# Conv stage of a two-layer decoder trunk: unit 3's weights made between the tiles of operand 6, and the squares of tiles 4 to 7 formed in pairs behind products 5 to 9

## The chip, the cores and the metric

The kernel runs as one program on one core of a Trainium2 chip. The metric is device time in microseconds (us), the median over runs. Before the change three runs took 2207.89, 2202.42 and 2208.22 us, so the median is 2207.89 us.

## What is computed

The reference is a decoder trunk of two layers in float32, with 1024 positions and a model width of 1024. The first layer mixes with a short gated convolution, the second with dilated attention, and a SwiGLU network follows each. Cut to what matters here:

```python
def rms_norm(x, g):
    y = x * lax.rsqrt(jnp.mean(x * x, axis=-1, keepdims=True) + EPS)
    return y * g

def short_conv_mixer(h, w_in, conv_k, w_out):
    b, c, u = jnp.split(h @ w_in, 3, axis=-1)
    y = depthwise_causal_conv(c * u, conv_k)          # 3 taps
    return (b * y) @ w_out

for i in range(2):
    h = rms_norm(x, mix_norm[i])
    x = x + (short_conv_mixer if i == 0 else dilated_attention)(h, ...)
    h = rms_norm(x, ffn_norm[i])
    x = x + (silu(h @ w_gate[i]) * (h @ w_up[i])) @ w_down[i]
return rms_norm(x, final_norm)
```

## The kernel before

**Operands.** Activations lie transposed: x is eight tiles X[0] to X[7] of 128 features by 1024 positions, each in two halves of 512 positions. Every float32 operand of a matmul is split in two: ScalarE makes the high half (a rounded copy, L138 for weights, L541 and L847 for activations) and VectorE the low half (the value minus the high half, L139, L542, L848). A product is taken as high times high, high times low, low times high, so each pair of 128-row blocks costs three matmuls of 128 by 512 (L549, L550, L551). The third of the three is the first that reads the weight's low half.

**Products.** The conv layer's first projection, x times `conv_w_in`, is done as Strassen products: unit u stands for a block of output columns, and for each unit seven products m = 1 to 7 are formed over four blocks of rows (12 matmuls). A method `products` walks a list of (unit, m) and records the matmuls; below, product n is the n-th of this list, counted from 0: (0,1) (1,1) (0,2) (1,2) (2,1) (2,2) (3,1) (3,2) (4,1) (4,2) (0,6) (1,6) (0,7) (1,7) (0,5) (1,5) (0,4) (1,4) (0,3) (1,3) (2,6) (2,5) (2,7), and so on. So product 6 is (3,1), 8 is (4,1), 10 to 13 are (0,6) (1,6) (0,7) (1,7), and 20 is (2,6). Products 1, 6, 7 and 4 of one unit add up in one PSUM bank. Behind m = 1, 6 and 7 the bank's value up to then is copied out by ScalarE (`save`, L555, written `part<-bank` in the profile), and the next product of that unit may not write to the bank before the copy is done.

**The order.** The schedule is the order of the code: each engine does its instructions in the order in which they are recorded. After product n is recorded, `start(n)` in `Conv.mix` records whatever else is put behind it: `ensure(self.at(u, m))` makes the split weights for everything up to (u, m), `combos` forms sums of weight blocks on VectorE (L186), `next(prep)` goes one step on in the generator `operands`, which makes the activation operands 1, 2, 6, 7, 5, 4, 3 (operand 6 is made in four tiles, two in each of two steps: L868, L869, L541, L542), and `self.squares` is the norm's share.

**The norm.** The products are formed with x that is only multiplied by the gain; the division by the root mean square comes later, so the sums of squares are needed only for what follows product 20. `summed` (L416 to L428) squares half a tile of X on ScalarE: tiles 0 and 1 go straight into two accumulators (L423), the others into a page `sq` (L427), and a DMA issued by GpSimd adds that half page to one of the two accumulators (L428, even tiles to one, odd tiles to the other). Two such DMAs on the same half of the same accumulator wait for one another. Hooks behind product 20 (`gather`) add the two accumulators on VectorE (`joined`, L431) and sum over the features with 16 small matmuls against ones (L461); those stand on TensorE between product 20 and product 21. `spread` behind (2,7) makes the scale.

Tiles live in 41 shared pages of 128 by 1024; a page that is taken again waits until its last reader is done, DMAs included. In the version before, the squares of tiles 0 to 3 are recorded behind product 0 (first half) and 4 (second half); those of tiles 4 to 7 stand in the list `late`, one half tile behind each product from 10 to 17. Unit 3's weights, `w<-raw` for (3,1) and (3,2), are made behind product 3, after all four tiles of operand 6.

Of the kernel before, what the change touches and what calls it, by code (L numbers as in the profile page):

```python
# [21 lines left out]
KT = D // 128  # L22
# [72 lines left out]
def trunk(ctx: ExitStack, tc: tile.TileContext, x, gains_in, cwi, ck, cwo, wqkv, wo, relb,  # L95
# [63 lines left out]
    def ensure(upto):  # L159
        while op_state[0] < min(upto + 1, len(ops)):  # L160
            key = ops[op_state[0] + 1][0] if op_state[0] + 1 < len(ops) else None
            if key in sums_of:
                sums_of.pop(key)()
            made[op_state[0]] = ops[op_state[0]][1]()
            op_state[0] += 1
# [191 lines left out]
    def run(*gens):  # L357
        for _ in zip(*gens):
            pass
        for g in gens:  # L360
            for _ in g:
                pass
# [12 lines left out]
    X = [None] * KT  # L375
# [459 lines left out]
    class Conv(Strassen):  # L835
# [166 lines left out]
        def mix(self, group1):  # L1002
            norm = self.norm
            prep = self.operands()
            stats = norm.stats(0, S)
            late = [(k, h) for h in range(2) for k in range(4, KT)]

            def start(n):
                if n == 0:
                    next(prep)  # L1010
                    ensure(self.at(2, 2))
                    self.squares(range(4), 0)
                elif n == 1:
                    next(prep)
                elif n == 2:
                    self.first(0)
                    next(prep)
                elif n == 3:
                    self.first(1)
                    ensure(self.at(3, 2))  # L1020
                    combos[CONV, 0](6)
                    ensure(self.at(4, 2))
                elif n == 4:
                    ensure(self.at(0, 6))
                    combos[CONV, 1](6)
                    ensure(self.at(1, 6))
                    self.squares(range(4), 1)
                elif n == 7:
                    next(prep)
                elif n == 8:  # L1030
                    ensure(self.at(1, 7))
                    self.first(2)
                elif n == 9:
                    self.first(3)
                    next(prep)
                    self.first(4)
                elif n == 10:
                    next(prep)
                    ensure(self.at(1, 5))
                elif n == 12:  # L1040
                    next(prep)
                    ensure(self.at(1, 4))
                elif n == 14:
                    next(prep, None)
                    ensure(self.at(1, 3))
                elif n == 18:
                    self.ahead = 3
                if n > 9 and late:
                    k, h = late.pop(0)
                    self.squares((k,), h)  # L1050
                    if h:
                        X[k] = None

            def gather():
                norm.joined()
                next(stats)

            def spread():
                run(stats)
                nc.scalar.activation(norm.acc, norm.rstd, AF.Square)  # L1060
                self.ready = True

            self.base = op_state[1]
            ensure(self.at(0, 1))
            next(prep)
            ensure(self.at(0, 2))
            self.run(start, {(2, 6): gather, (2, 7): spread})
            group1("co", self.plain, self.hid)

# [812 lines left out]
```

## Time and profile before

| what | value |
|---|---|
| median of three runs | 2207.89 us (2202.42 to 2208.22) |
| the profiled execution, its own time | 2207.41 us |
| span of the profile | 2205.6 us (1.8 us of the execution lie around it) |
| TensorE busy, share of the span | 2142.4 us, 97% |
| granted TensorE clock, mean | 0.986 of full |
| VectorE, ScalarE, GpSimd busy | 79%, 45%, 8% |
| moved over DMA | 265.03 MB, 120 GB/s on average |
| sum of squares DMAs (`acc<-sq`), conv stage | 12 of 256 KB |

All of the change lies in the first 90 us of the span. Times in the profile count from the span's start. In a timeline row stand the start, the duration, the engine, the line, the operation with its tiles, and in square brackets how long the engine stood idle before it and what ended that. PE is TensorE, DVE is VectorE, ACT is ScalarE, POOL is GpSimd, SP issues the loads.

### The profile page before, as it was taken

The page shows a single profiled execution, that of the slowest core. Times are in us where ns is not written, and L with a number is a line of the kernel's source. Part 1 is how long each engine was busy: PE and PEld are TensorE (multiplying, and loading weights), DVE is VectorE, ACT ScalarE, POOL GpSimd, SP SyncE. Part 2 cuts the span into 40 slices and gives each one's busy share as a digit, 9 for nine tenths or more (in the row PEclk, how much of TensorE's full clock was granted, in tenths as well). Part 3 has the DMA queues.
Part 4 walks back from the last instruction along what each step waited for, and adds up shares of the span by engine and source line. Part 5 has one row for each costly group of instructions (what it writes and reads, how often), then busy time and mean ns, then how long its engine had stood idle before and what let it go on. Part 6 is the DMA issues. An engine that isn't in the chain of part 4 may idle for free. (4 is left out here: it accounts for less than half of the span.)

```text
span 2205.6 us, 30628 instructions
## 1 busy us (share of the span) xinstructions
PE 2142.4 (97%) x11158; PEld 1830.9 (83%) x11158; DVE 1744.5 (79%) x3216; ACT 1000.9 (45%) x1812; POOL 180.9 (8%) x236
## 2 busy tenths in 40 slices
PE   8899999999999999999999999998999999999998
PEld 7688878778888878878999999886778888878887
DVE  7698758888888798865677777865888888889886
ACT  6433426444444544345545454534534444454435
POOL 1100001100101000010111111112000101000000
PEclk9999999999999999999999999998999999999999
DMA  5322543223233474323333333455223233265432
GB/s 183 91 74 80 204 154 86 98 94 105 106 104 112 133 269 151 111 67 132 85 91 99 93 96 99 138 168 161 71 77 103 103 106 111 99 233 194 156 93 77
DMA packets 137073, 265.03 MB, mean 120 GB/s; under 512 B 48520, under 2 KB 59800, under 8 KB 136922
## 3 DMA queue, kind: packets, MB, share of 16 engines
q1 hardware_dynamic: 75978, 184.80, 25.9%
q0 software_dynamic: 19776, 55.18, 7.7%
q10 hardware_dynamic: 41168, 23.10, 3.5%
q8 instruction: 88, 1.44, 0.3%
q14 instruction: 63, 0.52, 0.1%
HBM read 187.31 MB, written 66.27 MB: 115 GB/s over the span
## 5 line engine op out<-in xcount | busy, mean ns | idle before, releaser
L549 PE MATMUL bank<-b,w 128*128 128x512 f32 x1784 | 704.4, 395 | 16.3 <-ACT b L541 6.0
L551 PE MATMUL bank<-b,w 128*128 128x512 f32 x1784 | 700.5, 393 | 7.5 <-DVE w L139 7.5
L550 PE MATMUL bank<-b,w 128*128 128x512 f32 x1784 | 700.5, 393 | 0.6 <-DVE b L848 0.6
L549 PEld LDWEIGHTS bank<-b,w 128*128 128x128 f32 x1784 | 338.7, 190 | 91.4 <-ACT part L555 8.4
L551 PEld LDWEIGHTS bank<-b,w 128*128 128x128 f32 x1784 | 338.4, 190 | 82.5 <-DVE w L139 11.2
L550 PEld LDWEIGHTS bank<-b,w 128*128 128x128 f32 x1784 | 338.7, 190 | 70.1 <-DVE b L848 1.2
L138 ACT ACTIVATE w<-combo 128x512 fp32r<-128x512 f32 (+2 forms) x464 | 234.5, 535 | 295.5 <-DVE combo L186 287.2
L139 DVE TENSOR_TENSOR w<-combo,w 128x512 fp32r<-128x512 f32 (+2 forms) x464 | 260.2, 574 | 60.6 <-ACT w L138 58.6
L555 ACT ACTIVATE part<-bank 128x512 f32<-128x512 f32 x168 | 99.8, 594 | 263.9 <-PE bank L551 251.0
L139 DVE TENSOR_TENSOR w<-raw,w 128x512 fp32r<-128x512 f32 (+2 forms) x316 | 169.0, 559 | 16.4 <-ACT w L138 14.9
L559 DVE TENSOR_TENSOR part<-part,bank 128x256 f32<-128x256 f32 (+1 forms) x348 | 158.7, 485 | 28.3 <-PE bank L551 14.3
L138 ACT ACTIVATE w<-raw 128x512 fp32r<-128x512 f32 (+2 forms) x316 | 150.9, 520 | 47.4 <-PE bank L551 13.9
L770 DVE TENSOR_TENSOR x<-x,bank 128x512 f32<-128x512 f32 x168 | 114.2, 680 | 33.1 <-PE bank L551 32.8
L352 PE MATMUL bank<-w_hi,w 128*128 128x512 f32 (+1 forms) x320 | 121.3, 379 | 3.2 <-ACT w L138 3.2
L354 PE MATMUL bank<-w_hi,w 128*128 128x512 f32 (+1 forms) x320 | 119.1, 372 | 0.9 <-DVE w L139 0.9
L353 PE MATMUL bank<-w_lo,w 128*128 128x512 f32 (+1 forms) x320 | 118.8, 371 | 0.0
L482 DVE TENSOR_TENSOR x<-x,bank 128x512 f32<-128x512 f32 (+1 forms) x104 | 66.1, 642 | 65.5 <-PE bank L354 57.2
L352 PE MATMUL bank<-h_hi,w_hi 128*128 128x512 f32 x256 | 104.5, 408 | 0.1
L186 DVE TENSOR_TENSOR combo<-raw 128x512 f32<-128x512 f32 (+1 forms) x160 | 102.9, 643 | 0.0
L354 PE MATMUL bank<-h_hi,w_lo 128*128 128x512 f32 x256 | 100.2, 391 | 0.7 <-DVE w_lo L139 0.5
L353 PE MATMUL bank<-h_lo,w_hi 128*128 128x512 f32 x256 | 99.9, 390 | 0.0
L1156 ACT ACTIVATE part<-part 128x512 f32<-128x512 f32 x66 | 39.7, 627 | 106.0 <-DVE part L559 106.0
(258 smaller groups left out, 3854.2 us busy)
## 6 DMA issues: line engine op xcount, KB each, us to landing
hin<-part SPq DMA_DIRECT2D x126, 256.0 KB
raw<-in_ffn_w_gate SPq DMA_DIRECT2D x44, 512.0 KB
raw<-in_ffn_w_up SPq DMA_DIRECT2D x44, 512.0 KB
part<-sum POOLq DMA_DIRECT2D x72, 256.0 KB, 2.7
raw<-in_ffn_w_down SPq DMA_DIRECT2D x48, 384.0 KB
x<-spill SPq DMA_DIRECT2D x24, 512.0 KB
raw<-in_attn_w_qkv SPq DMA_DIRECT2D x24, 512.0 KB
raw<-in_conv_w_in SPq DMA_DIRECT2D x21, 512.0 KB
```

The source lines that it names most:

```text
L138: nc.scalar.activation(hi, src, AF.Copy)
L139: eng.tensor_tensor(out=lo, in0=src, in1=hi, op=ALU.subtract)
L186: eng.tensor_tensor(out=c, in0=a, in1=b, op=op)
L352: nc.tensor.matmul(b, whi[:, a], ahi[:, s], start=first, stop=False)
L353: nc.tensor.matmul(b, whi[:, a], alo[:, s], start=False, stop=False)
L354: nc.tensor.matmul(b, wlo[:, a], ahi[:, s], start=False, stop=last)
L549: nc.tensor.matmul(b, hi[:, a], bhi, start=start and k == 0, stop=False, skip_group_check=True)
L550: nc.tensor.matmul(b, hi[:, a], blo, start=False, stop=False, skip_group_check=True)
L551: nc.tensor.matmul(b, lo[:, a], bhi, start=False, stop=k == n - 1, skip_group_check=True)
L555: nc.scalar.activation(t, b, AF.Copy)
L559: nc.vector.tensor_tensor(out=t, in0=t, in1=b, op=ALU.add)
L770: nc.vector.tensor_tensor(out=X[n][:, half(h)], in0=X[n][:, half(h)], in1=b, op=ALU.add)
```

## The change

Three things in `start` of `Conv.mix` move; no arithmetic, no tile size and no DMA is added or removed. The rest of the kernel is the same, four lines shorter, so a line number above 1050 is four smaller in the changed kernel.

```diff
-            late = [(k, h) for h in range(2) for k in range(4, KT)]
-
...
                 elif n == 2:
                     self.first(0)
+                    ensure(self.at(3, 2))
                     next(prep)
                 elif n == 3:
                     self.first(1)
-                    ensure(self.at(3, 2))
                     combos[CONV, 0](6)
                     ensure(self.at(4, 2))
...
                 elif n == 14:
                     next(prep, None)
                     ensure(self.at(1, 3))
+                    X[:] = [None] * KT
                 elif n == 18:
                     self.ahead = 3
-                if n > 9 and late:
-                    k, h = late.pop(0)
-                    self.squares((k,), h)
-                    if h:
-                        X[k] = None
+                if n in (5, 6, 8, 9):
+                    self.squares(*{5: ((4, 5), 0), 6: ((6, 7), 0), 8: ((4, 5), 1), 9: ((6, 7), 1)}[n])
```

Unit 3's weights come between the second and the third tile of operand 6. On ScalarE this reads as follows; `w<-raw` are the high halves of weights (of the four in a row before, the first two are unit 3's, the others unit 4's), `b<-t_331` to `b<-t_334` the four tiles of operand 6, and the `part<-bank` at the end is the copy behind product 4.

```order
 L541 ACTIVATE b<-t_331 128x512
 L541 ACTIVATE b<-t_332 128x512
+L138 ACTIVATE w<-raw 128x512 x2
 L541 ACTIVATE b<-t_333 128x512
 L541 ACTIVATE b<-t_334 128x512
-L138 ACTIVATE w<-raw 128x512 x4
+L138 ACTIVATE w<-raw 128x512 x2
 L555 ACTIVATE part<-bank 128x512
```

The two high halves for unit 3 move ahead of two tiles, and unit 4's stay where they were. On VectorE the two low halves for unit 3 go ahead of the third and fourth tile of operand 6 too, directly behind the addition L559.

```order
 L542 TENSOR_TENSOR b<-t_331,b 128x512
 L559 TENSOR_TENSOR part<-part,bank 128x512
+L139 TENSOR_TENSOR w<-raw,w 128x512 x2
 L868 SCALAR_TENSOR_TENSOR t_329<-x,gains,t_329 128x512
 L869 SCALAR_TENSOR_TENSOR t_333<-x,gains,t_329 128x512
```

They moved past eight VectorE operations (the two L868, the two L869, three L542 and one L559); what stands behind those eight keeps its place in the list.

The squares: on ScalarE, from the squares of tiles 2 and 3 (second half) on, the kernel before has this. The three `part<-bank` rows are the copies behind products 6, 8 and 10; `b<-t_327` to `b<-t_330` are operand 7; `w<-combo` are the weights of products 12 and 13; L847 makes operand 5.

```order
L427 ACTIVATE sq<-x 128x512 x2
L555 ACTIVATE part<-bank 128x512
L541 ACTIVATE b<-t_327 128x512
L541 ACTIVATE b<-t_328 128x512
L541 ACTIVATE b<-t_329 128x512
L541 ACTIVATE b<-t_330 128x512
L555 ACTIVATE part<-bank 128x512
L138 ACTIVATE w<-combo 128x512 x2
L555 ACTIVATE part<-bank 128x512
L847 ACTIVATE b<-x,gains 128x512 x4
```

The changed kernel has this at the same place.

```order
L427 ACTIVATE sq<-x 128x512 x4
L555 ACTIVATE part<-bank 128x512
L427 ACTIVATE sq<-x 128x512 x2
L541 ACTIVATE b<-t_327 128x512
L541 ACTIVATE b<-t_328 128x512
L541 ACTIVATE b<-t_329 128x512
L541 ACTIVATE b<-t_330 128x512
L555 ACTIVATE part<-bank 128x512
L138 ACTIVATE w<-combo 128x512 x2
L427 ACTIVATE sq<-x 128x512 x4
L555 ACTIVATE part<-bank 128x512
L847 ACTIVATE b<-x,gains 128x512 x4
```

Eight half tiles of squares now stand here: two and two around the copy behind product 6, and four between the weights of product 13 and the copy behind product 10. The later places, behind products 10 to 17, are empty of squares. The eight accumulating DMAs on GpSimd keep their number and order, and GpSimd has no other work in this stage; the loads on SP keep their order.

## The prediction

> **What bounds the kernel now.** I read the page first, then the list of TensorE's waits, then the timeline of each engine over the first 90 us, and last the granted clock in windows.
>
> ```profile
> PE 2142.4 (97%) x11158; PEld 1830.9 (83%) x11158; DVE 1744.5 (79%) x3216; ACT 1000.9 (45%) x1812; POOL 180.9 (8%) x236
> ...
> PE bank L461 <- DVE acc L431: 7.4, 1, 7.4
> PE bank L549 <- ACT w L138: 3.2, 1, 3.2
> ```
>
> TensorE is busy for 97% of the span, so the end moves only when TensorE's pauses shrink or grow. Two of its longest lie where the change is. The timeline of TensorE shows them, and the pace beside them:
>
> ```profile
> 27.73 0.50 PE L549 MATMUL bank<-b,w 128*128 128x512 f32 x1 [3.15 <-ACT w L138]
> 32.85 0.39 PE L549 MATMUL bank<-b,w 128*128 128x512 f32 x1
> 35.59 0.39 PE L549 MATMUL bank<-b,w 128*128 128x512 f32 x1
> 38.31 0.39 PE L549 MATMUL bank<-b,w 128*128 128x512 f32 x1
> ...
> 46.47 0.39 PE L549 MATMUL bank<-b,w 128*128 128x512 f32 x1
> 49.19 0.41 PE L549 MATMUL bank<-b,w 128*128 128x512 f32 x1
> ...
> 79.20 3.57 PE L461 MATMUL bank<-ones,acc 128*128 128x1 f32 x16 [7.38 <-DVE acc L431]
> 82.63 0.77 PE L549 MATMUL bank<-b,w 128*128 128x512 f32 x1
> ```
>
> Product 6 starts at 27.73, product 7 at 32.85, 8 at 35.59, 9 at 38.31, 12 at 46.47, 13 at 49.19. A product at full pace takes 38.31 - 35.59 = 2.72, a matmul 0.227. At 79.20 come the norm's matmuls.
>
> **Part 1, unit 3's weights.** These rows of ScalarE, VectorE and SP carry it:
>
> ```profile
> 21.82 0.63 ACT L541 ACTIVATE b<-t 128x512 fp32r<-128x512 f32 x1 [0.69 <-DVE t L869]
> ...
> 27.06 2.17 ACT L138 ACTIVATE w<-raw 128x512 fp32r<-128x512 f32 x4
> ```
>
> ```profile
> 22.31 0.68 DVE L559 TENSOR_TENSOR part<-part,bank 128x512 f32<-128x512 f32 x1
> ...
> 28.39 1.28 DVE L139 TENSOR_TENSOR w<-raw,w 128x512 fp32r<-128x512 f32 x2
> ...
> 30.92 1.29 DVE L139 TENSOR_TENSOR w<-raw,w 128x512 fp32r<-128x512 f32 x2
> ```
>
> ```profile
> 9.86 4.85 SPq L1696 DMA_DIRECT2D x<-in_x  x8
> 15.02 1.00 SPq L1712 DMA_DIRECT2D raw<-in_conv_w_in  x2
> ...
> 15.00:20.00 5.00, 5.00 (x24) 4.14 (x23) 2.93 (x5) 5.00 (x11) 1.78 (x2) 1.00 1.05 411
> ```
>
> Four high halves in 2.17 are 0.52 apart. Behind the tile at 21.82 the two of unit 3 start at 22.34 and 22.86 and end by 23.5; their low halves follow L559 at about 23.0 and 23.6 and end by 24.3. TensorE asks at 27.73 - 3.15 = 24.58, so the wait goes. The load is no obstacle by the rows: 512 KB issued at 15.02 behind 2 MB of x (8 of 256 KB) are 2.6 MB, at 411 GB/s 6.4 us, so there at about 21.4 even if nothing of it had moved before. Product 6 took 32.85 - 24.58 = 8.27 instead of 2.72 (the wait, a short wait for the low half, and matmuls at half pace): **5.5 us come back**.
>
> What is late next: VectorE is full here, and the two low halves only trade places with tiles 3 and 4. Unit 4's low half still starts at 30.92, plus 0.1 for a later answer from ScalarE, and ends at 31.7. TensorE now asks for it at 24.58 + 2 x 2.72 + 0.45 = 30.5: **a new wait of 1.2 us** in product 8. Product 11 then ends at 31.7 + 10 x 0.227 + 3 x 2.72 = 42.1, which is 4.3 ahead of the 46.47 at which product 12 began.
>
> **Part 2, squares ahead of a copy.** Product 12, (0,7), adds to the bank whose value ScalarE must first copy out (L555 behind product 10). The new squares stand ahead of that copy.
>
> ```profile
> 34.17 1.14 ACT L423 ACTIVATE acc<-x 128x512 f32<-128x512 f32 x2
> ...
> 36.73 2.18 ACT L541 ACTIVATE b<-t 128x512 fp32r<-128x512 f32 x4
> ...
> 40.57 0.63 ACT L138 ACTIVATE w<-combo 128x512 fp32r<-128x512 f32 x1 [0.66 <-DVE combo L186]
> 43.95 0.60 ACT L555 ACTIVATE part<-bank 128x512 f32<-128x512 f32 x1 [2.75 <-PE bank L551]
> 44.44 2.56 ACT L847 ACTIVATE b<-x,gains 128x512 fp32r<-128x512 f32 x4
> ```
>
> ```profile
> 37.38 2.50 DVE L542 TENSOR_TENSOR b<-t,b 128x512 fp32r<-128x512 f32 x4 [2.04 <-ACT b L541]
> 39.79 0.69 DVE L186 TENSOR_TENSOR combo<-raw 128x512 f32<-128x512 f32 x1
> ```
>
> Before, ScalarE stood idle for 2.75 ahead of the copy: it had time, but the order decides. Now four squares of 0.52 come ahead of operand 7, which starts at 36.73 + 2.1 + 0.1 = 38.9. VectorE follows 0.65 behind at 39.5, reaches the weight sum 2.41 later at 41.9, and ScalarE's second weight comes 0.78 behind that at 42.7. Then stand the four other squares, 0.52 + 4 x 0.52, and the copy runs from 45.3 to 45.9. TensorE waits from 42.1 to 45.9: **a new wait of 3.8 us**; of the 4.3 gained 0.5 is left.
>
> **Part 3, the accumulating DMAs.** The fourth L847 of operand 5 takes the page of the squares of tiles 4 and 5 (second half), so it waits until their two DMAs have landed; behind it on ScalarE are two weights and the copy that product 13 waits for.
>
> ```profile
> 36.12 1.71 POOL L428 DMA_DIRECT2D acc<-sq  x2 [16.89 <-ACT sq L427]
> ...
> 66.68 1.73 POOL L428 DMA_DIRECT2D acc<-sq  x2 [8.23 <-ACT sq L427]
> 70.73 0.85 POOL L428 DMA_DIRECT2D acc<-sq  x1 [2.32 <-DMA acc<-sq]
> 74.62 0.84 POOL L428 DMA_DIRECT2D acc<-sq  x1 [3.04 <-DMA acc<-sq]
> ```
>
> Time from issue to landing, minimum, median and maximum: between 30 and 66 us, between 65 and 80 (beside loads of weights), and between 10 and 30 (beside the first loads):
>
> ```profile
> DMA to landing us min/median/max: 3.2/3.4/4.1
> DMA to landing us min/median/max: 3.2/4.1/6.9
> DMA to landing us min/median/max: 8.4/9.4/10.4
> ```
>
> Alone one takes 3.2; the second of a pair, issued 0.55 later, takes 4.1, so it lands 1.4 behind the first. Taking 1.4 as the spacing in a queue (an estimate from these rows), the pairs at 36.2 land at 39.4 and 40.8, the next pair at 42.2 and 43.6; the third pair must wait for those (0.5 to react, an estimate from 70.73 against 66.68 + 3.2) and lands at 45.9 and 47.3; the pair that matters is queued behind it and lands at 48.7 and 50.1. Then 0.61 for L847, 2 x 0.52 for the weights, and the copy ends at 52.4. Product 13 starts there instead of at 49.19: **3.2 late**. Its ends: without queueing (3.2 and 4.1 from issue at 44.7) 50.9, so 1.7 late; with 6.9 for every one, about 55.2, so 6 late. No load runs between 30 and 60 in that stretch of the order, so I take 52.4.
>
> **Part 4, the norm.** The last DMA was issued at 74.62 and L431 waited for it. Now all have landed by 54, and the 6.9 beside the loads is gone.
>
> ```profile
> 77.92 1.23 DVE L431 TENSOR_TENSOR acc<-acc,acc 128x1024 f32<-128x1024 f32 x1 [2.37 <-DMA acc<-sq]
> ...
> 1019.16 1.84 PE L461 MATMUL bank<-ones,acc 128*128 128x1 f32 x16
> ```
>
> Product 20 ends at 52.4 + 8 x 2.72 = 74.2. VectorE has eight operations (4.9 us) between the end of product 18 at 68.9 and L431, so L431 ends at 75.1, and TensorE's L461 starts there, **4.1 ahead** of 79.20. At full clock its 16 matmuls take 1.84, not 3.57: **1.7**. And at 82.63 to 86.59 the matmuls ran at half clock, which lost **2.0**:
>
> ```profile
> 83.17:86.59 3.42, 3.42 (x9) 2.64 (x8) 3.29 (x6) 1.05 (x2) 0.00 (x0) 0.50 0.00 0
> ...
> 407.44:410.85 3.41, 1.50 (x7) 0.96 (x6) 3.38 (x8) 0.85 (x2) 0.54 (x1) 1.00 0.58 231
> 410.85:414.27 3.42, 3.42 (x9) 2.63 (x9) 3.38 (x7) 0.30 (x1) 0.00 (x0) 0.50 0.00 0
> ...
> 1967.33:1970.75 3.42, 1.65 (x13) 1.68 (x14) 3.42 (x9) 1.68 (x3) 0.00 (x0) 1.00 1.03 392
> 1970.75:1974.20 3.45, 3.45 (x17) 2.84 (x16) 3.42 (x9) 0.28 (x1) 0.00 (x0) 1.00 1.04 403
> ```
>
> The columns are busy time of TensorE first and the granted clock third from last. A window of 3.41 us with 1.50 busy is followed by one at half clock, one with 1.65 is not; a half window costs 1.7. In the change three pauses can trigger one. Around product 12, TensorE works for 2.7 to 4.4 of the 10.3 us up to 52.4; a half window ahead of 52.4 is hidden by the copy, one that reaches past it costs up to 1.7 (I take 1.2). At the norm, 0.9 of waiting and 1.8 of L461, which seems to count as idle, make 2.8; in about three of four positions more than 1.8 of that falls into one window (1.3). At full clock throughout the sum is 4.1 + 1.7 + 2.0 = 7.8 gained; with these two, **5.3**. Freeing X[4] to X[7] earlier costs nothing: SP's list is the same and its loads wait for readers of weights.
>
> The Trainium skill, "TensorE: Matmul & The Clock Gate", section "What's actually happening", says that the default is half clock, that it returns after at least one idle window of about 3.4 us, and that the windows run free of the kernel. The row with 1.50 busy disagrees: a window that was 44% busy was enough.
>
> **From there to the end.** Later waits on TensorE are released by engines that follow TensorE's own products, so I carry the 5.3 through: 2207.41 - 5.3 = 2202.1 for the profiled execution, 0.5 below the median, hence about 2202.5 for the median. 0.3%, about what a measurement of this kernel can tell from no change, is 6.6 us, or 2201.3.
>
> **The rivals.**
> - *The clock stays up.* If no window is halved, or the DMAs land unqueued (1.5 better), the gain is 7.8 to 9.3: 2198.6 to 2200.1. For it: the positions of windows vary. Against it: both pauses together exceed two windows. The Trainium skill's rule of a whole idle window would favour this case, since pauses of 3.8 and 2.8 seldom hold one. 0.39.
> - *The squares' DMAs are slow in a burst.* At 6.9 each, product 13 starts at 55.2 and 2.8 more is lost: gain 2.5, 2204.9. For it: the burst is five pairs in 9 us. Against: 3.4 is the median with no loads beside. 0.09, still within 0.3%.
> - *Slower than before.* The page of those squares holds up ScalarE, and with it product 13, from the point at which each takes over about 8.3 us (between the 6.9 above, which loses 2.8, and 10.4): at 10.4, the trace's worst, the pairs land at 47, 58 and 59, product 13 starts at 61.5, 9.1 later than I take, and the end is 3.8 later plus one or two half windows, 2213 to 2215. Against: that maximum stood beside the first loads at 411 GB/s. 0.05.
> - *It doesn't do what it says*: unit 3's weights land late. Then part 1 gains less, but ScalarE's order in parts 2 and 3 sets product 13 anyway. It changes the sum by under 1.
>
> **How the numbers follow.** The forecast, a gain of 3.5 to 6.6, has 0.46; with the slow burst and the last rival (0.01) inside, same has 0.55, faster 0.39, slower 0.06 (0.05, and 0.01 for chance in later windows). The three runs before spread over 5.8 us, so one more half window or less on either side stays in the range: 2197 leaves out the best tenth, 2207.5 the slow cases.
>
> **What would show it.** Right: in the timeline after, no wait at product 6; a wait of 1 to 1.5 at product 8 for `w` L139; one of 3.5 to 4 at product 12 and one at product 13, both for ACT `part` L555; L461 at 74 to 77 behind VectorE alone, not a DMA. Wrong: no wait at product 12 (the copy isn't held up), L461 before 72 (gain over 9), or L549 waits over 5 us at product 13.

## The result and the profile after

| | median of the runs | ratio to before, 95% interval |
|---|---|---|
| before | 2207.89 us (20 runs, 2202.42 to 2209.72) | |
| the change | 2199.46 us (20 runs, 2192.21 to 2203.39) | 0.9965 (0.9956 to 0.9973) |
| the change once more (g1 below) | 2195.87 us (6 runs), before beside it 2207.35 (14 runs) | 0.9954 (0.9939 to 0.9969) |

The ratio of the first comparison is a gain of 7.7 us, between 6.0 and 9.7. That is faster, by a little more than the 6.6 us below which I had called it the same; the interval reaches down across that line.

The profiled execution of the change took 2192.98 us, 14.4 less than that of before. Not all of this is the change: I separate it below. In the profile after, the rows that answer to those of before are TensorE's busy time and its waits by releaser over the whole span (us in total, times, longest):

```profile
PE 2135.2 (97%) x11158; PEld 1824.9 (83%) x11158; DVE 1744.8 (80%) x3216; ACT 1000.1 (46%) x1812; POOL 181.4 (8%) x236
...
PE bank L549 <- ACT part L555: 11.2, 6, 3.5
...
PE bank L461 <- DVE acc L431: 0.8, 1, 0.8
```

TensorE's busy time fell from 2142.4 to 2135.2 with the same 11158 matmuls: busy time also shrinks when fewer of them run at half clock. The longest wait for L431 fell from 7.4 to 0.8, the one of 3.2 for `w` L138 is gone, and the waits for ScalarE's copy L555 have grown, from 5.9 us in four over the whole span to 11.2 in six. TensorE's timeline shows where:

```profile
30.75 0.50 PE L551 MATMUL bank<-b,w 128*128 128x512 f32 x1 [1.31 <-DVE w L139]
45.01 0.50 PE L549 MATMUL bank<-b,w 128*128 128x512 f32 x1 [3.54 <-ACT part L555]
51.44 0.50 PE L549 MATMUL bank<-b,w 128*128 128x512 f32 x1 [1.82 <-ACT part L555]
75.93 1.95 PE L461 MATMUL bank<-ones,acc 128*128 128x1 f32 x16 [0.81 <-DVE acc L431]
77.74 0.48 PE L549 MATMUL bank<-b,w 128*128 128x512 f32 x1
```

These are product 8 (its third matmul), product 12, product 13 and the norm. No wait stands at product 6. ScalarE's timeline shows why products 12 and 13 wait:

```profile
33.25 1.14 ACT L423 ACTIVATE acc<-x 128x512 f32<-128x512 f32 x2
34.30 2.18 ACT L427 ACTIVATE sq<-x 128x512 f32<-128x512 f32 x4
36.38 0.57 ACT L555 ACTIVATE part<-bank 128x512 f32<-128x512 f32 x1
36.86 1.14 ACT L427 ACTIVATE sq<-x 128x512 f32<-128x512 f32 x2
37.90 2.18 ACT L541 ACTIVATE b<-t 128x512 fp32r<-128x512 f32 x4
...
42.30 2.17 ACT L427 ACTIVATE sq<-x 128x512 f32<-128x512 f32 x4
44.38 0.57 ACT L555 ACTIVATE part<-bank 128x512 f32<-128x512 f32 x1
45.00 2.16 ACT L847 ACTIVATE b<-x,gains 128x512 fp32r<-128x512 f32 x3
49.14 0.72 ACT L847 ACTIVATE b<-x,gains 128x512 fp32r<-128x512 f32 x1 [1.98 <-DMA acc<-sq]
49.77 1.13 ACT L138 ACTIVATE w<-combo 128x512 fp32r<-128x512 f32 x2
50.81 1.06 ACT L555 ACTIVATE part<-bank 128x512 f32<-128x512 f32 x2
```

Eight squares stand ahead of operand 7 (L541 at 37.90), four of them those of tiles 4 to 7; four more stand ahead of the copy at 44.38, and the fourth L847 waits 1.98 for a DMA that still reads its page. VectorE idles for operand 7, 4.12 us against 2.04 before, and finds the sums landed at L431:

```profile
38.55 2.50 DVE L542 TENSOR_TENSOR b<-t,b 128x512 fp32r<-128x512 f32 x4 [4.12 <-ACT b L541]
...
74.66 1.22 DVE L431 TENSOR_TENSOR acc<-acc,acc 128x1024 f32<-128x1024 f32 x1
```

**What is the change's, and what is one execution's.** I compare matmuls by their number from the start: the 85th, ahead of product 6, and the 349th, behind the norm. Their rows before come first, those after second:

```profile
22.60 0.39 PE L550 MATMUL bank<-b,w 128*128 128x512 f32 x1
...
99.05 0.39 PE L551 MATMUL bank<-b,w 128*128 128x512 f32 x1
```

```profile
21.57 0.39 PE L550 MATMUL bank<-b,w 128*128 128x512 f32 x1
...
92.29 0.39 PE L551 MATMUL bank<-b,w 128*128 128x512 f32 x1
```

The 85th comes 1.03 us earlier after the change, by the first loads, in code that the change doesn't touch (I call this the start-up). So the stage gained 99.05 - 92.29 - 1.03 = 5.7 us. From there to the last matmul the code is the same, and yet 8.0 us more were saved. Windows of half clock fall otherwise there: half clock lasted 62.8 us over the whole of one profile and 38.3 of the other. In the second profile of the change the stage gained 7.3 and the part behind it 7.7. In the thirteen profiles beside that of before, the part behind the norm took between 0.6 us more and 8.0 us less than in it, in no order that follows from what the kernels changed: 0.1 less in experiment e1 below, 2.4 less in e2, whose norm stands where the change's does, 3.4 and 2.7 less in two profiles of one kernel. The profiled execution of the change was itself a fast one, 6.5 us under the median of its twenty runs and the second fastest of them, while that of before lay 0.5 under its median. So most of the 8.0 is that execution's, not the change's.

### The profile page after: what moved, and what is told of

The parts are those of the page before. It is cut to its first block, busy times and chain, and to the rows that moved or that the text cites. A ratio compares the mean times of both kernels' runs of the same rounds, so it can differ in the third digit from the quotient of the medians.

```text
span 2191.2 us, 30626 instructions
## 1 busy us (share of the span) xinstructions
PE 2135.2 (97%) x11158; PEld 1824.9 (83%) x11158; DVE 1744.8 (80%) x3216; ACT 1000.1 (46%) x1812; POOL 181.4 (8%) x236
## 5 line engine op out<-in xcount | busy, mean ns | idle before, releaser
L549 PE MATMUL bank<-b,w 128*128 128x512 f32 x1784 | 702.4, 394 | 16.4 <-ACT part L555 11.2
L138 ACT ACTIVATE w<-combo 128x512 fp32r<-128x512 f32 (+2 forms) x464 | 234.5, 535 | 297.4 <-DVE combo L186 291.5
L139 DVE TENSOR_TENSOR w<-combo,w 128x512 fp32r<-128x512 f32 (+2 forms) x464 | 261.0, 576 | 56.3 <-ACT w L138 54.3
L555 ACT ACTIVATE part<-bank 128x512 f32<-128x512 f32 x168 | 99.7, 594 | 259.7 <-PE bank L551 248.6
L139 DVE TENSOR_TENSOR w<-raw,w 128x512 fp32r<-128x512 f32 (+2 forms) x316 | 169.5, 561 | 16.9 <-ACT w L138 15.4
L559 DVE TENSOR_TENSOR part<-part,bank 128x256 f32<-128x256 f32 (+1 forms) x348 | 159.3, 489 | 27.1 <-PE bank L551 16.2
L138 ACT ACTIVATE w<-raw 128x512 fp32r<-128x512 f32 (+2 forms) x316 | 150.6, 519 | 45.6 <-PE bank L551 14.1
```

Of the source, the lines that this page charges most:

```text
L138: nc.scalar.activation(hi, src, AF.Copy)
L139: eng.tensor_tensor(out=lo, in0=src, in1=hi, op=ALU.subtract)
L549: nc.tensor.matmul(b, hi[:, a], bhi, start=start and k == 0, stop=False, skip_group_check=True)
L555: nc.scalar.activation(t, b, AF.Copy)
L559: nc.vector.tensor_tensor(out=t, in0=t, in1=b, op=ALU.add)
```

## The experiments

My theory: the gain comes from the norm alone, whose sums now land early; the wait won at product 6 is used up by ScalarE's copies, because what sets their time (VectorE's work on operand 7, the squares, the page) doesn't depend on TensorE. The rival: the parts add up, and the weights are worth their 4.3 us. A second question is the clock: what the two halved windows in my sum are worth.

"Stage" below is the gain at the 349th matmul against the 85th, in the profiled execution, as above (added matmuls not counted). It is one execution's figure, with the half clock that fell into it.

| label | what it is | stage | ratio to before (interval) | median |
|---|---|---|---|---|
| e1 | weights alone | -2.4 | 0.9997 (0.9984 to 1.001) | 2204.52 |
| e2 | squares alone | 4.2 | 0.9966 (0.9953 to 0.9978) | 2198.92 |
| the change | both | 5.7, 7.3 | 0.9965, 0.9954 | 2199.46, 2195.87 |
| e3 | both, second-half squares later | 8.0 | 0.9973 (0.9961 to 0.9986) | 2200.37 |
| v1 | all late squares behind the copy | 1.8 | 0.9983 (0.9972 to 0.9995) | 2201.62 |
| f1 | before, late squares left out | 7.6 | 0.995 (0.9933 to 0.9968) | 2194.02 |
| f2 | the change, late squares left out | 9.2 | 0.9938 (0.9926 to 0.9951) | 2192.6 |
| f3 | before, 28 matmuls ahead of the norm | 1.7 | 0.9985 (0.9975 to 0.9996) | 2203.17 |
| g4 | before, 32 matmuls ahead of the norm | 3.4 | 0.9969 (0.9958 to 0.9981) | 2198.17 |
| v2, g2 | first tiles' squares early | 10.4, 8.7 | 0.9941, 0.9942 | 2192.48, 2192.68 |
| g3 | the same without early weights | 8.3 | 0.9951 (0.9938 to 0.9965) | 2197.12 |

### e1: the weights alone

```diff
                 elif n == 2:
                     self.first(0)
+                    ensure(self.at(3, 2))
                     next(prep)
                 elif n == 3:
                     self.first(1)
-                    ensure(self.at(3, 2))
```

> Unit 3's weights made between the tiles of operand 6, and the squares of tiles 4 to 7 left one by one behind products 10 to 17, as before. Theory (the parts don't add up: the gain of the first is used up by whatever is next in line): the wait at product 6 goes and TensorE is 4 to 5 us ahead at products 7 to 11, but VectorE has no idle time from product 8 to 14 and its low halves for product 14 (L139 at 51.35 before) come no earlier, so TensorE waits 2 to 4 us in all for L139 or L555 between products 12 and 15 and is at most 1.5 us ahead behind product 15; the norm's wait for the DMAs stays at 7 us or grows. Gain 0 to 2 us against before, so 2206 to 2208 by the median. Rival (the parts add up): the 4.3 us of the weights stay to the end, 2203.5, with L461 4 us ahead of 79.2.

No gain: 2204.52 against 2206.91, ratio 0.9997. The timelines of TensorE and VectorE in e1:

```profile
31.35 0.50 PE L551 MATMUL bank<-b,w 128*128 128x512 f32 x1 [1.33 <-DVE w L139]
48.17 0.79 PE L549 MATMUL bank<-b,w 128*128 128x512 f32 x1 [3.37 <-ACT part L555]
...
81.11 3.57 PE L461 MATMUL bank<-ones,acc 128*128 128x1 f32 x16 [7.31 <-DVE acc L431]
```

```profile
37.07 2.50 DVE L542 TENSOR_TENSOR b<-t,b 128x512 fp32r<-128x512 f32 x4 [2.04 <-ACT b L541]
...
42.74 2.49 DVE L884 TENSOR_TENSOR x<-x 128x512 f32<-128x512 f32 x4
```

TensorE ran ahead, and gave it back in one wait of 3.37 at product 13. VectorE's L542 starts at 37.07 where it started at 37.38 before: nothing on its side moved, so L884, L847 behind it and the copy came when they always came. The norm still waits 7.31. With the start-up of 0.45, product 13 starts at 48.6, 0.6 ahead of the 49.19 of before: that is what is left of a lead of 4.1 at product 12. My theory held in this, but for the place: I had named the low halves for product 14 or the copy, and it was the copy for product 13, which ScalarE does behind L847. Two windows of half clock (47.55 to 54.38) around that wait then cost 3.0 over products 13 and 14, which put the stage 2.4 behind before in this execution, the slowest of the twelve runs. The median lies 1.5 under the 2206 to 2208 that I gave and nearer to the rival's 2203.5; but the interval, a gain of 3.5 at most, leaves out the rival's 4.3, and L461 is not ahead.

### e2: the squares alone

```diff
                 elif n == 2:
                     self.first(0)
-                    ensure(self.at(3, 2))
                     next(prep)
                 elif n == 3:
                     self.first(1)
+                    ensure(self.at(3, 2))
```

(against the change)

> The squares formed in pairs behind products 5, 6, 8 and 9, and unit 3's weights left behind product 3, as before. Theory: product 13's start is set by ScalarE's chain of squares, operand and copy and by the page of the squares, whatever TensorE did ahead of it; so the wait of 3 us at product 6 is back, the one at product 12 is under 1 us, product 13 still starts at 51 to 53.5, and the norm comes as early as in the whole change (L461 at 75 to 77, behind VectorE). Gain 5 to 8 us, within 1.5 us of the whole change. Rival (the parts add up): without the weights 4.3 us of the whole change's gain are gone, so a gain of 3.5 us or less, and L461 at 79 or later.

0.9966, where the whole change has 0.9965. TensorE's timeline in e2:

```profile
27.31 0.50 PE L549 MATMUL bank<-b,w 128*128 128x512 f32 x1 [3.15 <-ACT w L138]
...
51.95 0.61 PE L549 MATMUL bank<-b,w 128*128 128x512 f32 x1 [2.97 <-ACT part L555]
...
76.44 1.95 PE L461 MATMUL bank<-ones,acc 128*128 128x1 f32 x16 [0.81 <-DVE acc L431]
```

The wait of 3.15 is back, the one at product 12 is gone, and product 13 starts at 51.95 + 0.42 (start-up) = 52.4, in the change at 52.5 in both profiles. The norm stands at 76.9 by the same reckoning, in the change at 77.0 and 75.4. The stage of 4.2 is 1.5 short of the change's 5.7, and one more window of half clock accounts for it: in e2 one follows the norm (79.49 to 82.91, worth 1.7), in the change none. So no worth of the weights shows in this change, and what it gains comes from the squares; the intervals of the two leave some 3 us either way. The theory held, and the rival's L461 at 79 or later didn't come.

### e3 and v1: squares behind the copies

e3, against the change:

```diff
-                if n in (5, 6, 8, 9):
-                    self.squares(*{5: ((4, 5), 0), 6: ((6, 7), 0), 8: ((4, 5), 1), 9: ((6, 7), 1)}[n])
+                if n in (5, 6, 11, 13):
+                    self.squares(*{5: ((4, 5), 0), 6: ((6, 7), 0), 11: ((4, 5), 1), 13: ((6, 7), 1)}[n])
```

> The whole change, but the second half of the pairs of squares is formed behind products 11 and 13 in place of 8 and 9, so behind the copy L555 that product 12 waits for. Theory: the wait of 3.5 us at product 12 is the price of the two pairs' place on ScalarE (2.2 us) and on the page; it falls to 1 to 2 us, product 13 waits under 1 us for L555, VectorE's low halves (L139) or L431 are next, and the norm still comes behind VectorE, not behind a DMA. L461 at 73 to 75, 1.5 to 3 us ahead of the whole change, by clock windows between 0 and 4 us faster than it. Rival (the wait at product 12 is not the squares' place but VectorE's pace): L555 comes no earlier, the norm waits for the later DMAs again, and the time is that of the whole change or longer.

The wait at product 12 fell to 1.45, L461 came at 73.88, with the start-up 2.3 and 0.7 us ahead of the change's two profiles, and the page's wait at the fourth L847 was gone. But product 13 still waited, and longer than I expected:

```profile
43.20 0.50 PE L549 MATMUL bank<-b,w 128*128 128x512 f32 x1 [1.45 <-ACT part L555]
49.40 0.50 PE L549 MATMUL bank<-b,w 128*128 128x512 f32 x1 [3.19 <-ACT part L555]
```

Its copy stands behind L847 and two weights, and those behind L884 on VectorE, as in e1 (here the profile names no releaser of L847; by the times it starts when the first L884 has ended). Over the runs e3 can't be told from the change: a stage better by 0.7 to 2.3 us lies inside the two intervals.

v1, against the change (X is let go behind product 15):

```diff
                 elif n == 4:
...
-                    self.squares(range(4), 1)
...
                 elif n == 8:
...
+                    self.squares(range(4), 1)
...
-                if n in (5, 6, 8, 9):
+                if n in (11, 12, 13, 15):
```

> Unit 3's weights as in the change; the second half of the squares of tiles 0 to 3 is moved from product 4 to behind product 8, and the pairs of tiles 4 to 7 to products 11, 12, 13 and 15, so that ScalarE makes operand 7 ahead of them. Theory: VectorE's idle 2 to 4 us ahead of operand 7's low halves (L542 at 37.38 before, 38.55 in the change) shrink to under 1, the copy for product 12 comes in time, TensorE waits under 2 us in all between products 8 and 14, and the norm's L431 finds the DMAs landed (last issued near 58). L461 at 71 to 74, a gain of 9 to 13 us against before, 1 to 5 us faster than the whole change. Rival (VectorE is full and its low halves of unit 5 to 7 set the pace from product 8 on): the waits move to L139 at products 14 and 15 and L461 stays at 75 to 77, the time within 1 us of the whole change.

A miss: the stage gained only 1.8. L542 did start at 34.13, without a wait, and product 12 didn't wait. But ScalarE then stood for the squares' own DMAs:

```profile
44.86 1.15 ACT L138 ACTIVATE w<-combo 128x512 fp32r<-128x512 f32 x2 [1.75 <-DMA acc<-sq]
...
65.19 0.63 ACT L138 ACTIVATE w<-combo 128x512 fp32r<-128x512 f32 x1 [3.84 <-DMA acc<-sq]
73.84 0.63 ACT L138 ACTIVATE w<-combo 128x512 fp32r<-128x512 f32 x1 [3.82 <-DMA acc<-sq]
```

A weight takes the page that a square has just left and waits until the DMA has read it. Before the change this was so too (L138 at 74.19, 3.07). By way of VectorE's low halves the second wait holds up product 19 by 1.83, and the third holds L431 up, for which TensorE waits 1.78 in place of 0.81. Half clock adds to it: it stands from 47.03 to 50.44, from 67.51 to 70.92 and from 77.75 to 84.58, behind the waits at products 13 and 19 and at the norm. So the page isn't the whole loss; the runs don't part it from the clock's share. L461 at 76.39 lies in the range that the rival gave, but the waits at products 14 and 15 that it named aren't there.

### f1 and f2: no late squares at all

The call of `self.squares` for tiles 4 to 7 is taken out, in f1 from the version before, in f2 from the change.

> The version before with the squares of tiles 4 to 7 and their eight DMAs left out (the sums of squares then lack these tiles); unit 3's weights behind product 3, as before. It shows how much of the stage hangs on those squares at all. Theory (the norm's wait for the DMAs and ScalarE's waits for their pages are what the change wins): product 6 still waits 3.1, L461 starts at 72.5 to 74.5 behind VectorE, 5 to 7 us ahead of 79.2, and runs at full pace; gain 6 to 10 us, no less than the whole change's 7.7. Rival (the squares only trade places with other work of ScalarE, and the norm is held by VectorE's own work): L461 at 76 or later, gain under 4 us.

> The whole change with the squares of tiles 4 to 7 and their eight DMAs left out (the sums of squares then lack these tiles). Against the kernel before without them it gives the worth of unit 3's weights alone where no square stands in the way. Theory: product 6 doesn't wait, product 8 waits 1.3, product 12 under 0.5, product 13 1.5 to 3 for L555, then VectorE's own work sets the norm: L461 at 70.5 to 72.5, 1.5 to 3 us ahead of the same without the early weights, not the 4.3 of the wait. Rival (the weights' 4.3 us were eaten by the squares alone): with them gone the whole 4.3 us stay, L461 4 to 5 us ahead of the same without the early weights.

In f1 the norm's L461 starts at 73.07, in f2 at 71.18, in both after a wait of 0.81 for VectorE's L431. So by the runs 11 us (0.995; 7 to 15 by the interval) hang on those squares, and the change's 7.7 are a good part of them. The early weights are worth at most 1.9 - 0.3 (start-up) = 1.6 us here, in the range of the theory, not 4.3; "at most", since f1 lost 1.5 us more in half clock at product 6 than before did.

### f3 and g4: the norm's clock by itself

Both are the version before, with matmuls whose result is overwritten put into the wait at the norm:

```diff
             b = bank()
+            if getattr(self, 'warm', None) is not None:
+                for _ in range(28):
+                    nc.tensor.matmul(b, self.warm[:, :128], self.warm, start=True, stop=True)
+                self.warm = None
             for t in range(nt):
```

(32 in g4; `warm` is set to the high half of an operand tile in `gather`)

> The version before with 28 matmuls of 128 by 512 more on TensorE ahead of the norm's L461 (their result is overwritten), to fill the 7.4 us in which it waits for L431; nothing else changes. It measures the clock's share of the norm by itself: 28 x 0.227 = 6.4 us of work. Theory (the half clock after the wait comes from TensorE's idle time): L461 starts at 79.2 as before, takes 1.84 in place of 3.57, the windows from 79.8 to 86.6 are granted 1.00, and the products behind are 3.7 us ahead of before: 2203 to 2205 by the median if the later windows are the same. Rival (the half clock has another cause, or L461 counts as idle whatever stands before it): half clock still stands behind L461 and the gain is under 1.5 us.

> The version before with 32 matmuls more ahead of L461 in place of 28, so that they end 0.1 us ahead of L461 or hold it up by a few tenths; their result is overwritten. With 28 the window up to 80.32 had 1.04 us of them and 1.5 us of L461, was 75% busy by the rows, and the next was halved all the same. Theory (the 16 one-column matmuls of L461 count as idle for the clock): now that window has 1.9 to 2 us of matmuls of 512 columns, and no window behind the norm is halved, or at most in one of four positions of the windows; 3 to 4 us ahead of before behind the norm in place of 2.0, 2202 to 2204 by the median. Rival (the halved window has nothing to do with what stood ahead): a half window follows L461 again, gain 2 us behind the norm as with 28.

With 28 half clock still followed; with 32 it didn't. TensorE's rows and the stretches behind them, first of f3, then of g4 (in the stretches TensorE's busy time is first, the granted clock third from last):

```profile
71.44 6.51 PE L462 MATMUL bank<-b 128*128 128x512 f32 x28
78.81 2.22 PE L465 MATMUL bank<-ones,acc 128*128 128x1 f32 x16 [0.85 <-DVE acc L431]
```

```profile
76.91:80.32 3.41, 2.56 (x19) 2.06 (x17) 1.23 (x1) 0.00 (x0) 0.00 (x0) 1.00 0.01 0
80.32:83.73 3.41, 3.41 (x11) 2.83 (x12) 2.33 (x5) 0.98 (x3) 0.00 (x0) 0.50 0.00 0
```

```profile
71.31 7.42 PE L462 MATMUL bank<-b 128*128 128x512 f32 x32
78.71 1.95 PE L465 MATMUL bank<-ones,acc 128*128 128x1 f32 x16
```

```profile
79.00:82.40 3.40, 3.40 (x23) 3.09 (x24) 1.37 (x3) 0.79 (x2) 0.00 (x0) 1.00 0.00 0
82.40:85.80 3.40, 3.40 (x16) 2.81 (x16) 2.03 (x4) 0.63 (x1) 0.00 (x0) 1.00 0.02 5
```

In f3 the clock's window up to 80.32 is busy for 2.56 by the rows, 75%, and the next is halved. Of the 2.56 only 1.04 (76.91 to 71.44 + 6.51) are matmuls of 512 columns; the rest is the 16 of one column (L465 here, L461 before). f3's median lies in the range that I gave, but not for the reason that I gave. In g4 the added matmuls reach L465 without a gap, which runs in 1.95, and no half clock follows. The windows lie otherwise there than I had expected: counted in steps of 3.413 from the half window at 28.53, their edges are at 76.32, 79.73 and 83.15, so the two stretches shown straddle them, and the two windows around the norm hold 2.4 and 2.6 us of 512-column matmuls, not 1.9 to 2. g4 thus shows what a busy TensorE is worth at the norm, but the part of the one-column matmuls rests on f3 and on the rows in the last section.

The 349th matmul of g4 is 3.94 us ahead of before, of which 0.49 stood at the norm's start already (78.71 against 79.20): 3.45 behind it, against the 1.7 + 2.0 = 3.7 of my sum. That term is shown. The runs gained 6.8 (4.2 to 9.3), more than the stage, and their median lies nearly 4 under the 2202 to 2204 that I gave.

### v2, g2 and g3: squares of the first tiles early

ScalarE's idle 2.3 and 1.4 us behind unit 3's weights (22 to 27 us) take the four squares of tiles 0 to 3, and of those of tiles 4 to 7 only one pair stands ahead of operand 7. Against the change:

```diff
                 elif n == 2:
                     self.first(0)
                     ensure(self.at(3, 2))
+                    self.squares(range(4), 1)
                     next(prep)
...
                 elif n == 4:
...
-                    self.squares(range(4), 1)
...
-                if n in (5, 6, 8, 9):
-                    self.squares(*{5: ((4, 5), 0), 6: ((6, 7), 0), 8: ((4, 5), 1), 9: ((6, 7), 1)}[n])
+                if n in (5, 8, 11, 13):
+                    self.squares(*{5: ((4, 5), 0), 8: ((6, 7), 0), 11: ((4, 5), 1), 13: ((6, 7), 1)}[n])
```

> Unit 3's weights as in the change; the second half of the squares of tiles 0 to 3 is moved forward from product 4 to product 2 (behind unit 3's weights, where ScalarE stood idle 2.3 and 1.4 us), and the pairs of tiles 4 to 7 stand behind products 5, 8, 11 and 13, so that one square pair in place of four pairs stands ahead of operand 7. Theory: VectorE's idle 4.1 us ahead of L542 shrink to about 1, L542 starts near 35.5 in place of 38.55, product 12 waits under 0.5 for L555, product 13 under 2, ScalarE waits for no page of squares, L461 at 70 to 72.5; gain 9 to 13 us against before, 2 to 5 us more than the whole change. Rival (VectorE's own work sets the norm): L542 comes earlier, but L461 stays at 74 to 76 and the time is within 1 us of the whole change.

2192.48 us, 0.9941 (0.9928 to 0.9955), a gain of 13 us. TensorE and VectorE in v2:

```profile
46.63 0.50 PE L549 MATMUL bank<-b,w 128*128 128x512 f32 x1 [2.44 <-ACT part L555]
71.14 1.95 PE L461 MATMUL bank<-ones,acc 128*128 128x1 f32 x16 [0.81 <-DVE acc L431]
```

```profile
35.39 2.50 DVE L542 TENSOR_TENSOR b<-t,b 128x512 fp32r<-128x512 f32 x4 [1.00 <-ACT b L541]
```

L542 starts at 35.39 in place of 38.55 and product 12 doesn't wait. The norm stands at 71.14, with the start-up of 1.10 at 72.2; f2, without any late square, has it at 71.18 + 0.74 = 71.9: here the late squares cost 0.3 that the profile shows. I expected under 2 us of wait at product 13; it was 2.44.

> The changed kernel once more, on the same chip and day as the three beside it, to see which of its trace's rows are the kernel's and which are one execution's luck. Theory (the stage gains 5 to 6 us, the rest of the 14 us between the first two profiled executions lies in half-clock windows that fall otherwise from run to run): the waits at products 8, 12 and 13 and L461 come within 0.5 us of the first profile of the change (1.3, 3.5, 1.8, L461 at 76 to 77), the number of half windows differs by 1 to 4, and the time is 2197 to 2202. Rival (the change itself removes half windows far behind the stage): the profile again shows about 38 us of half clock and a time near 2193.

> The version with the squares of tiles 0 to 3 behind product 2 and the pairs of tiles 4 to 7 behind products 5, 8, 11 and 13, once more beside the change on the same chip. Theory: 4 to 6 us faster than the change by the median (2193 to 2196 against 2198 to 2201), ratio to before 0.993 to 0.9955, L461 at 70.5 to 72. Rival (its first five runs were lucky): within 2 us of the change.

> The same placing of the squares as in the version beside it, but unit 3's weights behind product 3 as before. Theory (early weights are worth something only where no copy of ScalarE stands behind them): the wait of 3.1 at product 6 is back, product 12 and 13 hardly wait, product 13 starts at 48 to 49.5 in place of 46.6, L461 at 72 to 74: 1.5 to 3 us slower than with the early weights, 2195 to 2198. Rival (TensorE's lead is worth nothing in any order, VectorE alone sets the norm): L461 at 70.5 to 71.5, no difference; or the whole 4.3 us are lost.

On one chip, v2's code (g2) has 2192.68 and 0.9942 (0.9926 to 0.9958), the change (g1) 2195.87 and 0.9954 (0.9939 to 0.9969). The medians are 3.2 apart, less than the 4 to 6 that I expected, and the intervals overlap. Over all their runs, on more than one chip, v2 has 2192.5 (11 runs) and the change 2199.4 (26 runs). The profiles agree better: with the start-up the norm stands at 72.2 and 72.3 in v2's two (g2's L461 is at 73.37, with a start 1.07 later than that of before, past the 70.5 to 72 that I gave), and at 77.0 and 75.4 in the change's two.

g1's waits are 1.34, 3.49 and 0.97 (1.82 in the first profile), L461 at 74.71, 1.3 ahead of what I expected. Its median lies under the 2197 to 2202 that I gave, and its half clock of 42.4 us and its span of 2190.3 are near those that the rival named, so this profile doesn't refute it. The two profiles of one code also lie close together in the part behind the norm, 8.0 and 7.7 for the change, 3.4 and 2.7 for v2. What speaks against the rival is that g1's profiled execution, too, was the fastest of its six, 3.8 under their median, and that the runs of one code differ widely with the granted clock: those of before go from 2198.49 us at a mean clock of 0.990 to 2210.92 at 0.985. That some of the gain behind the norm is the change's own is not ruled out.

Without the early weights (g3) L461 stands at 72.39, with the start-up at 72.8, and the median at 2197.12, 4.4 above g2, with ratios (0.9951 and 0.9942) whose intervals overlap. By the norm's start the weights are worth some 0.5 us in this order; that they pay is not shown by the runs.

## Why the prediction was right, and where its size was off

- **Part 1** held. The wait at product 6 went, product 8 waits 1.31 for `w` L139 (I had 1.2). Product 12 asks at 45.01 - 3.54 + 1.03 (start-up) = 42.5; I had 42.1.
- **Part 2** held: 3.54 at product 12 against 3.8, for `part` L555, with the eight squares ahead of operand 7 and the four behind it as in the working.
- **Part 3** held: the fourth L847 waits for the DMA, product 13 starts at 51.44 + 1.03 = 52.5 against 52.4. The second profile has 51.84 + 0.67 = 52.5.
- **Part 4** held in its mechanism. L431 waits for no DMA, L461 runs at full pace, no half clock follows. It starts at 75.93 + 1.03 = 77.0 in the first profile and 74.71 + 0.67 = 75.4 in the second; I had 75.1. The first lost 1.6 in a half window from 52.36 that reached past product 13.
- **The step that was off** is "with these two, 5.3". The sum at full clock was 7.8; I took off 1.2 for a half window at products 12 and 13 and 1.3 for one at the norm. Measured in the two profiles: 1.6 and none at product 13, none and none at the norm. So the stage gained 5.7 and 7.3; 7.8 less these losses would be 6.2 and 7.8, and of the 0.5 missing in both, 0.3 is an L461 that came later than the sum says and 0.1 its longer run (1.95). The runs gained 7.7 (6.0 to 9.7), nearer to 7.8 than to 5.3. The price of a half window (1.7) was right; that the two would come nearly each time was not. At the norm it is a matter of position: of the ten profiles in this study whose norm waits under 2 us with no matmuls added, six have a half window within 5 us behind L461, both of the change's have none. That none came in either is thus partly luck of the position.

The forecast of 2202.5 us is thus 3 us above the measured median, and the case that gave the measured number is the rival that I had at 0.39, the clock that stays up (2198.6 to 2200.1). That rival's reason was only half right: in both profiles a half window did come around products 12 and 13, the norm alone was spared. So the agreement of its number is in part luck; the runs also gained more than the stage shows (see below). The rival "slower" needed DMAs of over 8 us, and those of the page had landed by 49.14 + 1.03 = 50.2, where the spacing of 1.4 put 50.1. That the squares alone give the whole gain (e2) fits the working, too: there product 13's start is set by ScalarE's order and the page, not by the weights.

What stays open: almost every kernel here gained more over its runs than its stage shows (e2 7.5 and 4.2, g4 6.8 and 3.4), by 1.6 to 4.5 us; only e3 gained less. All are compared with the one profile of before, which may have had a better stage than most of its runs. No second profile of before was taken.

## What to carry to other kernels

Before a wait is removed, follow the next thing that its engine needs from an engine that works in order, and ask what sets the time of that: e1's 4 us of lead shrank to 0.6 at the copy for product 13, whose time VectorE set. Work that is needed late but can be done early belongs in an idle stretch of its engine ahead of the critical operand, not only away from the end: v2 also moved the squares of tiles 0 to 3 forward, and its stage gained 10.4 and 8.7 against the change's 5.7 and 7.3. And two single profiles, of kernels that differ only ahead of it, can differ by 8 us in code that nobody touched, so count a change's gain between two matmuls around it, not at the end.

## What the runs showed of the hardware

- **One-column matmuls didn't hold the clock up.** In f3 a window 75% busy by the rows, more than half of that with 128x1 matmuls, was followed by half clock. g2 shows the same more sharply: its window with the norm is busy for 3.22 of 3.42 us, but 1.95 of that are the 16 matmuls of one column, and the next window is halved:

```profile
73.17:76.59 3.42, 3.22 (x22) 3.00 (x23) 1.05 (x4) 2.10 (x4) 0.00 (x0) 1.00 0.00 0
76.59:80.00 3.41, 3.41 (x9) 2.67 (x9) 2.49 (x4) 0.63 (x1) 0.00 (x0) 0.50 0.00 0
```

  It is one of six windows, 75 to 94% busy by the rows, that hold the norm's one-column matmuls and were followed by half clock. In the change's second profile (g1) the window from 74.63 holds the same 16 with 1.53 us of 512-column matmuls in place of g2's 1.41, and full clock follows. The Trainium skill, "TensorE: Matmul & The Clock Gate", section "What's actually happening", lets half clock return after at least one idle window; by that rule f3's window, with 1.04 us of 512-column matmuls in it, would not have been one. The trace disagrees.
- **A partly idle window was enough for half clock.** Counted over the fourteen profiles by windows of 3.413 us at full clock, those with the norm's 16 matmuls left out: all 91 that were under 42% busy were followed by half clock, 22 of 29 between 42 and 49%, one of 45 between 49 and 60%, and none of 8561 above. The row with 1.50 us (44%) in the prediction lies in the part where either happens: in the change's first profile the window from 400.52 has 1.50 too, and full clock follows.
- **Half clock can hold on through a window more than half busy.** In the second profile of the change (g1), a window with 1.94 us of TensorE's work is followed by another at half clock:

```profile
43.91:47.33 3.42, 1.94 (x5) 1.56 (x6) 3.42 (x7) 3.27 (x6) 2.13 (x3) 0.50 1.04 188
47.33:50.74 3.41, 3.41 (x9) 2.25 (x7) 2.79 (x5) 1.40 (x4) 1.62 (x2) 0.50 0.72 130
50.74:54.15 3.41, 2.44 (x11) 1.93 (x11) 3.41 (x6) 2.23 (x6) 0.07 (x1) 1.00 0.64 116
```

- **The windows' position is an execution's own.** Their edges lie at 45.53 in one profile of the change and at 43.91 in the other, no multiple of 3.41 apart; the Trainium skill, "TensorE: Matmul & The Clock Gate", section "What's actually happening", says that they run free of the kernel, and the trace agrees. The part behind the norm took from 0.6 us more to 8.0 less than before; in the same part half clock lasted from 23.9 us (the change's first profile) to 41.0 (before), so much of this goes with the windows.
